# Gated delta rule as a scan of transition matrices, with the output projection's tiles in another order

## The chip, the cores and the metric

The kernel runs on one core of a Trainium2 chip. The metric is the device time of one execution in microseconds (us), lower is better. The core has a matrix engine (PE), a vector engine (DVE), a scalar engine (ACT), a GpSimd engine (POOL), and queues that start transfers (DMA), the main one on SP. Each engine runs its own list of instructions in order, and waits on semaphores for the others. Matrix products are written to PSUM banks; the kernel holds four banks with the tag `g` (psg) and four with the tag `m` (psm).

## What is computed

One layer of a hybrid decoder on 1024 tokens of width 1024, in float32: normalise, project, four mixers A to D of 256 channels each, an output projection added to x, then a SwiGLU block and a last normalisation. The change concerns mixer C, a gated delta rule in 16 chunks of 64 tokens and 4 heads, and what follows it.

```python
def chunk_gated_delta_rule(q, k, v, g, beta):
    ...
    kb = k * beta[..., None]
    low = jnp.where(strict, jnp.einsum('bhncd,bhnsd->bhncs', kb, k) * decay, 0.0)
    rhs = jnp.concatenate([v * beta[..., None], kb * jnp.exp(gc)[..., None]], axis=-1)
    sol = lax.linalg.triangular_solve(low, rhs, left_side=True, lower=True, unit_diagonal=True)
    u, w = sol[..., :dv], sol[..., dv:]
    ...
    def step(state, inp):
        qg_n, w_n, u_n, attn_n, kd_n, dec_n = inp
        v_new = u_n - jnp.einsum('bhcd,bhde->bhce', w_n, state)
        o = jnp.einsum('bhcd,bhde->bhce', qg_n, state) + jnp.einsum('bhcs,bhse->bhce', attn_n, v_new)
        state = state * dec_n[..., None, None] + jnp.einsum('bhcd,bhce->bhde', kd_n, v_new)
        return state, o
...
    mix = jnp.concatenate([y_a, y_b.astype(x.dtype), y_c, y_d], axis=-1)
    x = x + (mix @ w_out[l]).astype(x.dtype)
    x = x + swiglu(rmsnorm(x, norm2_w[l]), w_gate_up[l], w_down[l]).astype(x.dtype)
```

## The kernel before

Channels lie on the 128 partitions and tokens on the free axis, in two halves of 512 tokens. A large product is float32 made of three passes (`mm3`, L178 to L180): both operands are split into a rounded part and a rest (`wh` and `wl` for weights, made by ACT at L167 and DVE at L169; `mh` and `ml` for the mixers' outputs, L886 and L887). Such a pass is a matmul of 128x128 weights on 512 columns and is called a full matmul below. A column of weights is a generator in `queue`; `fill(us)` lets the queue put in some steps of three full matmuls, so that small work is interleaved with them. In which order the instructions then stand on each engine is decided when the program is built; the lists in the section on the change are from that order.

Mixer C needs small matmuls: 64x64, float32, on half of the partitions. Each is two records in the trace. Before the scan, a triangular inverse `Ti` is made per head and chunk: DVE solves blocks of 32 by substitution (L852, L853), transfers rearrange them (L868), and two sets of 32x32 matmuls (L932, L944) join them.

The scan (L1024 to L1078) goes through 16 chunks in turn. In each, PE multiplies the keys with the state (L1034), DVE adds the scaled result to the values (L1038), PE applies `Ti` (L1045), DVE copies the result (L1047), PE multiplies with the decayed keys (L1054) and makes two products per output (L1066, L1067), and DVE updates the state (L1060). That is up to 20 small matmuls in three places per chunk, 308 in all, with `fill(0.64)` after each place. The keys in channel order (`Kc`) come from a copy in DRAM (`dK`), which ACT's queue writes and POOL's queue reads.

The output projection is split: columns `o0` and `o1` (`col_out`, 8 per half, 18 full matmuls each, evacuated at L916) use the six blocks of mixers A, B and D and run beside the scan; columns `p0` and `p1` (`col_out2`, 4 per half, 2 x 6 full matmuls, evacuated at L983) add the two blocks of mixer C. After chunk 8 the first half's output is normalised (`onorm`, L591 to L613) and `p0` is put in the queue. Behind the scan come the statistics of the first half (`stats`, L152, with sums of squares in `acc2` that DVE adds at L989) and the split of the first half for the SwiGLU block (`split_h0`, L1017).

The SwiGLU block is done with Strassen-like products whose right sides are sums and differences of quarters of x. `sums_b(j)` (L1175 to L1184, lower parts at L1168) makes the sides T1, T2 and T4 from columns j and j+4 of both halves, and `sums_b2(j)` those of T3 and of the last quarter. The string `GQ` sets the order: n waits for a column, s and t are the sums, a and b are four products that need no sums. The first product that needs a sum is S2 of the first block. It reads T2, and weights that DVE makes (L1237) and ACT splits (L1120).

POOL multiplies `vtok` and `ktok` by per-token factors (L840), four instructions of 128x1024.

## Time and profile before

| | us |
|---|---|
| median of 3 runs | 1191.02 |
| lowest and highest run | 1187.15, 1191.15 |
| the profiled execution | 1191.06 |
| span of its trace | 1189.3 |
| PE busy | 1149.8 (97%) |
| DVE busy | 837.6 (70%) |
| ACT busy | 497.5 (42%) |
| POOL busy | 292.2 (25%) |

The span is from the first to the last instruction; 1.8 us of the profiled execution lie around it. Columns of the views: in a timeline, start, duration, engine, line, operation, output and input, count, and in brackets the idle time before it with what ended it. Matmuls overlap, so the distance of two starts, not the duration, is what one costs. [...]

### The profile page before, as it was taken

To read this page: it belongs to the slowest core of one execution; us is meant where nothing else is said; L and a number is where in the kernel's file an instruction comes from. 1 tells how busy PE (TensorE), PEld (TensorE's weight loads), DVE (VectorE), ACT (ScalarE), POOL (GpSimd) and SP (SyncE) were. 2 spreads that over 40 slices of the span, in tenths; PEclk is the share of its full clock that TensorE was granted. 3 is DMA by queue.
4 is the path that set the end of the run, shared out by engine and by line. 5 is a ranking of instruction groups with operands and counts; after the bars stand their busy time and mean duration, and the time that the engine had idled before them with its cause. 6 is when DMAs were issued, how large, how long until landed. Compare 5 with 4: busy or idle time off the path is not lost.

```text
span 1189.3 us, 17008 instructions
## 1 busy us (share of the span) xinstructions
PE 1149.8 (97%) x6426; PEld 931.0 (78%) x6426; DVE 837.6 (70%) x1419; ACT 497.5 (42%) x852; POOL 292.2 (25%) x232
## 2 busy tenths in 40 slices
PE   7999999989999899997999999999999999999996
PEld 6877777877787667775888888888888888888885
DVE  7656445377499346799866676576665679999876
ACT  7465335455322323457323233232323335436553
POOL 5200000011000200001275566465565510000004
PEclk9999999999999899998999999999999999999998
DMA  6121101211222712352132222131222299555103
GB/s 218 54 82 36 37 19 55 70 53 36 59 66 64 256 45 90 98 163 87 66 119 82 76 85 107 53 107 53 106 89 89 77 330 354 177 186 183 39 1 142
DMA packets 64115, 122.19 MB, mean 103 GB/s; under 512 B 16105, under 2 KB 22553, under 8 KB 64033
## 3 DMA queue, kind: packets, MB, share of 16 engines
q1 hardware_dynamic: 45488, 95.00, 24.4%
q10 hardware_dynamic: 16912, 20.34, 4.7%
q0 software_dynamic: 1632, 5.77, 1.3%
q8 instruction: 51, 0.84, 0.3%
q14 instruction: 32, 0.25, 0.1%
HBM read 98.48 MB, written 22.59 MB: 102 GB/s over the span
## 4 chain that ended last, share of the span: by engine, by line
PE 85%; DVE 8%; ACT 3%; DMA 2%; issue 1%; SPq 0%; DVEq 0%; ACTq 0%
PE psg L178 17%; PE psg L180 17%; PE psg L179 17%; PE psm L178 9%; PE psm L179 8%; PE psm L180 8%; ACT S L365 1%; DMA wr<-w_out 1%; DVE wl L169 1%; DMA t<-x 1%; DVE big L222 1%; PE psm L159 1%; PE psm L591 1%; DVE S L852 1%; PE psm L569 1%
## 5 line engine op out<-in xcount | busy, mean ns | idle before, releaser
L178 PE MATMUL psg<-big,wh 128*128 128x512 f32 x616 | 251.8, 409 | 1.0 <-ACT wh L167 1.0
L180 PE MATMUL psg<-big,wl 128*128 128x512 f32 x616 | 245.5, 399 | 4.9 <-DVE wl L169 4.9
L179 PE MATMUL psg<-big,wh 128*128 128x512 f32 x616 | 245.7, 399 | 0.3 <-DVE big L222 0.3
L180 PEld LDWEIGHTS psg<-big,wl 128*128 128x128 f32 x616 | 117.5, 191 | 32.1 <-DVE wl L169 6.4
L178 PEld LDWEIGHTS psg<-big,wh 128*128 128x128 f32 x616 | 117.5, 191 | 29.9 <-issue 4.1
L179 PEld LDWEIGHTS psg<-big,wh 128*128 128x128 f32 x616 | 117.8, 191 | 23.5 <-DVE big L222 0.8
L1121 DVE TENSOR_TENSOR wl<-S,wh 128x512 fp32r<-128x512 f32 x115 | 94.8, 834 | 28.2 <-ACT wh L1120 27.9
L167 ACT ACTIVATE wh<-wr 128x512 fp32r<-128x512 f32 (+2 forms) x104 | 58.3, 564 | 129.2 <-PE psg L179 98.5
L1120 ACT ACTIVATE wh<-S 128x512 fp32r<-128x512 f32 x115 | 70.7, 625 | 99.0 <-PE psm L179 36.3
L169 DVE TENSOR_TENSOR wl<-wr,wh 128x512 fp32r<-128x512 f32 (+2 forms) x104 | 64.3, 624 | 42.0 <-ACT wh L167 38.2
L1274 DVE TENSOR_TENSOR t<-t,t 128x512 f32<-128x512 f32 x44 | 41.9, 956 | 43.5 <-ACT t L1148 30.5
L1224 POOL TENSOR_TENSOR wr<-S 128x512 f32<-128x512 f32 x20 | 28.9, 1448 | 176.4 <-DVE r L146 158.3
L1298 POOL TENSOR_TENSOR t<-t,rstdb 128x512 f32<-128x512 f32 x40 | 55.4, 1407 | 37.1 <-DVE t L1294 37.1
L1495 POOL TENSOR_TENSOR big<-big,t 128x256 f32<-128x256 f32 (+1 forms) x9 | 8.0, 917 | 196.0 <-ACT t L1490 196.0
L1120 ACT ACTIVATE yB<-S 128x512 fp32r<-128x512 f32 x55 | 33.0, 623 | 48.0 <-PE psm L180 31.5
L1121 DVE TENSOR_TENSOR yA<-S,yA 128x512 fp32r<-128x512 f32 x51 | 40.0, 799 | 18.4 <-ACT yA L1120 17.8
L1121 DVE TENSOR_TENSOR yB<-S,yB 128x512 fp32r<-128x512 f32 x55 | 40.5, 758 | 14.7 <-ACT yB L1120 14.1
L1120 ACT ACTIVATE yA<-S 128x512 fp32r<-128x512 f32 x51 | 30.8, 623 | 48.0 <-PE psm L180 25.5
L1148 ACT ACTIVATE t<-t 128x512 f32<-128x512 f32 x22 | 13.9, 633 | 76.4 <-POOL t L1147 72.2
L1237 POOL TENSOR_TENSOR S<-S 128x512 f32<-128x512 f32 x20 | 26.8, 1341 | 74.6 <-DVE wl L1121 48.0
L1232 POOL TENSOR_TENSOR S<-wr,S 128x512 f32<-128x512 f32 x20 | 31.7, 1583 | 35.7 <-DVE wl L1121 26.3
L178 PE MATMUL psm<-big,wh 128*128 128x512 f32 x96 | 37.5, 391 | 0.0
(486 smaller groups left out, 2835.1 us busy)
## 6 DMA issues: line engine op xcount, KB each, us to landing
S<-w_gu SPq DMA_DIRECT2D x42, 512.0 KB, 3.7
wr<-w_in SPq DMA_DIRECT2D x48, 256.0 KB, 2.6
actd<-t ACTq DMA_DIRECT2D x22, 512.0 KB, 2.6
t<-w_down SPq DMA_DIRECT2D x22, 512.0 KB, 5.1
wr<-w_down SPq DMA_DIRECT2D x33, 256.0 KB, 3.9
wr<-w_out SPq DMA_DIRECT2D x24, 256.0 KB, 2.6
S<-actd SPq DMA_DIRECT2D x11, 512.0 KB, 6.1
big<-xd SPq DMA_DIRECT2D x4, 1024.0 KB, 8.7
```

Of the source, the lines that this page charges most:

```text
L167: act(hi, raw, AF.Copy)
L169: V.tensor_tensor(lo, raw, hi.bitcast(F32), SUB)
L178: mm(out, lhsT=w[0], rhs=hi, start=start, stop=False)
L179: mm(out, lhsT=w[0], rhs=lo, start=False, stop=False)
L180: mm(out, lhsT=w[1], rhs=hi, start=False, stop=stop)
L1120: act(hi, raw, AF.Copy)
L1121: V.tensor_tensor(lo, raw, hi.bitcast(F32), SUB)
L1224: early(f).tensor_tensor(r["S1"], r["A21"], r["A22"], ADD)
L1232: early(f).tensor_tensor(r["S2"], r["S1"], r["A11"], SUB)
L1237: early(f).tensor_tensor(r["S4"], r["A12"], r["S2"], SUB)
L1274: V.tensor_tensor(v[:, h, :], v[:, h, :], s[:, h, :], MUL)
L1298: early(f).tensor_tensor(v[:, h], v[:, h], rstdb[:, hs(h)], MUL)
```

## The change

The scan's state is made by one matrix per chunk: S(n+1) = M(n) S(n) + B(n), with M(n) = decay - W K and B(n) the offset. Five batches of 64 small matmuls each make these for all 32 pairs of heads and chunks at once: W (`Wc`), the solved values (in `vtok`), M (`Mt`), the offsets (in the states' tile `St`), and corrected queries (in `qg`). ACT evacuates three of them and DVE two, in groups of 128x512. The scan is then one product of 4 small matmuls and one DVE addition for each of 14 chunks, with one step of `fill`. The outputs of four chunks at a time are made by `outputs`, 28 or 32 small matmuls in one place. In all there are 500 small matmuls.

`dK` and its two transfers each way are gone. POOL multiplies `vtok` alone; DVE makes `K2`, `ktok` and `Mt`, two instructions of 128x1024 each, and a small identity (`id64`). The x tiles in the places S8 and S3 are loaded after the batches that use these places.

Of the output projection, `o0` runs beside the batches and the scan, then `p0`; the second half is done after that as eight columns `f1` (`col_all`, 24 full matmuls each, all eight blocks). `stats(0)` and `split_h0` stand under the first of them, and `sums_b` between them. The string `GQ` is changed for it.

```diff
-GM = (2.08, 2.64, 8.4, 3.56, 2.28)
-GS = (0.64, 0.64, 0.64)
+GM = (2.08, 2.64, 1.28, 2.56, 1.28)
+GS = (0.64,)
...
-GQ = 'n0 L0 s0 n1 n2 s2 q0 n3 a0 s1 L1 s3 t3 P0 a1 P1 t0 b0 t2 S0 b1 P2 t1'
+GQ = 'n0 s0 n1 s1 L0 n2 s2 q0 n3 a0 s3 L1 P0 a1 t0 P1 b0 t1 S0 b1 t2 P2 t3'
...
-    dK = dr.tile([2, P, T], F32, name="dK")
-    for hp in range(2):
-        nc.scalar.dma_start(out=dK[hp], in_=kq[hp][:, 0].rearrange("p n t -> p (n t)"))
...
-    for c in (slice(0, 16), slice(16, 32)):
-        for t, k in ((vtok, br), (ktok, kds)):
-            G.tensor_tensor(t[:, c, :], t[:, c, :], k[:, c].unsqueeze(2).broadcast_to([P, 16, 64]), MUL)
+    for c in groups:
+        G.tensor_tensor(vtok[:, c, :], vtok[:, c, :], by_tok(vtok, br, c), MUL)
...
+    def col_all(h, ct):
+
+        def steps(w):
+            p = psg()
+            for q, kt in enumerate(order + [4, 5]):
+                mm3(p, w(q), mh[h][:, kt, :], ml[h][:, kt, :], q == 0, q == 7)
+                if q == 5 and len(queue) > 1:
+                    queue[1].prep()
...
+            def evac():
+                add_x2(h, ct, p)
+                done_x2(h, ct)
...
     for ct in range(8):
         col_out(0, ct)
-    for ct in (0, 4, 1, 5, 2, 6, 3, 7):
-        col_out(1, ct)
+    K2 = S(8, [P, 32, 64])
+    for c in groups:
+        V.tensor_tensor(K2[:, c, :], ktok[:, c, :], by_tok(K2, nbeg, c), MUL)
+        V.tensor_tensor(ktok[:, c, :], ktok[:, c, :], by_tok(ktok, kds, c), MUL)
...
+    Mt = S(6, [P, 32, 64])
+    for c in groups:
+        V.tensor_tensor(Mt[:, c, :], bcu(id64, 16), by_tok(Mt, decC, c), MUL)
...
+    def batch(lhs, rhs, evac):
+        for g in range(4):
+            p = psm()
+            for q in range(8):
+                for r in half:
+                    mm(p[r, q * 64:(q + 1) * 64], lhsT=lhs[r, 8 * g + q, :], rhs=rhs[r, 8 * g + q, :],
+                       start=True, stop=True)
+            evac(g, p.rearrange("p (q c) -> p q c", c=64))
...
+    Wc = S(3, [P, 32, 64])
+    batch(Ti, K2, copy_to(Wc))
+    batch(Ti, vtok, copy_to(vtok))
     x_tile(S(8, [P, 2, T]))
+    fill(GM[3])
+    batch(Wc, ktok, add_to(Mt))
+    St = S(1, [P, 16, 2, 64])
...
+    batch(ktok, vtok, to_states)
+    batch(Wc, attnT, add_to(qg))
     x_tile(S(3, [P, 2, T]))
...
+    norm0 = onorm_steps(oC, 0, dnn, qs)
+    for n in range(1, 15):
+        p = psm()
+        for hp in range(2):
+            for r in half:
+                mm(p[r, hp * 64:(hp + 1) * 64], lhsT=Mt[r, hp * 16 + n, :], rhs=St[r, n, hp, :],
+                   start=True, stop=True)
+        V.tensor_tensor(St[:, n + 1], p[:, 0:P].rearrange("p (a c) -> p a c", a=2), St[:, n + 1], ADD)
+        if n in (3, 7, 11):
+            outputs(n // 4)
+        if n >= 8:
+            next(norm0, None)
+        fill(GS[0])
+    outputs(3)
...
+    split_c(0)
+    for j in range(4):
+        col_out2(0, j, len(queue))
+    onorm(oC, 1, dnn, qs, GO2)
+    split_c(1)
...
+    while queue:
+        step()
+    flush()
+    for ct in (0, 4, 1, 5, 2, 6, 3, 7):
+        col_all(1, ct)
+    queue[0].prep()
+    fill(2 * 0.64)
+    stats(0)()
+    for k in range(KT):
+        split_h0(k)
+        fill(0.64)
```

PE in the middle of the scan, before: the names are psg for a bank of the output projection, `big`, `wh`, `wl` for its operands, Sst for the state, t and vn for the values, S for the matrices.

```order
L1034 MATMUL psm_3744<-Sst_3721,S_538_3521 64x64 x4
L178 MATMUL psg_3717<-big_3297,wh_3686 128x512
L179 MATMUL psg_3717<-big_3298,wh_3686 128x512
L180 MATMUL psg_3717<-big_3297,wl_3688 128x512
L1045 MATMUL psm_3755<-t_586_3743,S_512_3287 64x64 x4
L178 MATMUL psg_3717<-big_3297,wh_3686 128x512
L179 MATMUL psg_3717<-big_3298,wh_3686 128x512
L180 MATMUL psg_3717<-big_3297,wl_3688 128x512
L1054 MATMUL psm_3777<-vn_3754,S_408_2385 64x64 x4
L1066 MATMUL psm_3742<-S_336_1961,Sst_3721 64x64
L1067 MATMUL psm_3742<-S_335_1960,vn_3754 64x64
```

The output products go on alternating behind these rows (L1066, L1067). The same place of the change (Mt and the states are both S tiles there):

```order
L176 MATMUL psg_3957<-big_3293,wh_3934 128x512
L177 MATMUL psg_3957<-big_3294,wh_3934 128x512
L178 MATMUL psg_3957<-big_3293,wl_3936 128x512
L1078 MATMUL psm_4010<-S_561_3781,S_530_3425 64x64 x4
L176 MATMUL psg_3957<-big_3293,wh_3934 128x512
L177 MATMUL psg_3957<-big_3294,wh_3934 128x512
L178 MATMUL psg_3957<-big_3293,wl_3936 128x512
L1078 MATMUL psm_4031<-S_561_3781,S_530_3425 64x64 x4
```

Three places of small matmuls per chunk, with outputs in the third, have become one, and the full matmuls between them are the same.

DVE ahead of product S2, before, from the evacuation of the last column of the projection (L983) on: wl and wr are weights, t and S the sums.

```order
L983 TENSOR_TENSOR S_540_3527<-psg_4878,S_540_3527 128x512
L989 TENSOR_TENSOR cB<-cB,t_840_4887 128x512
L1121 TENSOR_TENSOR wl_4925<-wr_4922,wh_4924 128x512
L1168 TENSOR_TENSOR S_815_4748<-t_827_4810,S_814_4747 128x512
L989 TENSOR_TENSOR cB<-cB,t_841_4892 128x512
L1121 TENSOR_TENSOR wl_4931<-wr_4928,wh_4930 128x512
L1224 TENSOR_TENSOR wr_4692<-praw_4689 128x512
L1175 SCALAR_TENSOR_TENSOR t_844_4911<-yA_3325,cA,t_844_4911 128x512
L1175 SCALAR_TENSOR_TENSOR t_851_4934<-yB_3328,cA,t_851_4934 128x512
L1176 SCALAR_TENSOR_TENSOR t_844_4911<-S_539_3524,cA,t_844_4911 128x512
L1183 SCALAR_TENSOR_TENSOR S_813_4746<-t_844_4911,S_812_4745 128x512
```

The sums for S2 go on behind these rows. DVE at the same place of the change, from the evacuation of the last f1 column (L921) on:

```order
L921 TENSOR_TENSOR S_570_3926<-psg_4927,S_570_3926 128x512
L1157 TENSOR_TENSOR wl_4997<-wr_4994,wh_4996 128x512
L1268 TENSOR_TENSOR praw_4634<-wr_4638,praw_4634 128x512
L916 TENSOR_TENSOR cB<-cB,t_767_4958 128x512
L1273 TENSOR_TENSOR praw_4634<-praw_4634 128x512
L1211 SCALAR_TENSOR_TENSOR t_770_4977<-yB_3324,cA,t_770_4977 128x512
L1157 TENSOR_TENSOR wl_5005<-praw_4634,wh_5004 128x512
L1212 SCALAR_TENSOR_TENSOR t_770_4977<-S_570_3926,cA,t_770_4977 128x512
L1219 SCALAR_TENSOR_TENSOR S_715_4678<-t_770_4977,S_714_4677 128x512
L1229 TENSOR_TENSOR t_783_5027<-t_783_5027 128x512
L1204 TENSOR_TENSOR S_713_4676<-t_770_4977,S_712_4675 128x512
```

In the first list 25 instructions stand from that L983 to the weights of S2 (L1237), in the second four from that L921 to them (L1273) and ten to the last lower part of T2 (the L1204 that writes S_713). On PE, 36 full matmuls stand between that column and S2 before, and 48 in the change.

DVE in the change where columns p0 end and the first f1 column begins (L921 evacuates, L916 adds squares, L167 makes the first weights of f1):

```order
L921 TENSOR_TENSOR yB_3324<-psg_4460,yB_3324 128x512
L916 TENSOR_TENSOR cB<-cB,t_663_4468 128x512
L921 TENSOR_TENSOR S_570_3926<-psg_4472,S_570_3926 128x512
L916 TENSOR_TENSOR cB<-cB,t_668_4486 128x512
L921 TENSOR_TENSOR yB_3324<-psg_4490,yB_3324 128x512
L916 TENSOR_TENSOR cB<-cB,t_670_4498 128x512
L921 TENSOR_TENSOR S_570_3926<-psg_4502,S_570_3926 128x512
L916 TENSOR_TENSOR cB<-cB,t_672_4510 128x512
L167 TENSOR_TENSOR wl_4528<-wr_4524,wh_4526 128x512
L916 TENSOR_TENSOR cB<-cB,t_673_4515 128x512
L916 TENSOR_TENSOR cB<-cB,t_674_4520 128x512
```

Before, the columns p0 stood among the scan's last chunks, and the weights that follow them were made beside it; now the weights of the first f1 column stand behind the last evacuation of p0.

## Rows read from the trace of the kernel before

**Rows 1.** The page: engines (busy, share, count); one group (busy, mean ns).

```profile
PE 1149.8 (97%) x6426; PEld 931.0 (78%) x6426; DVE 837.6 (70%) x1419; ACT 497.5 (42%) x852; POOL 292.2 (25%) x232
...
L1121 DVE TENSOR_TENSOR wl<-S,wh 128x512 fp32r<-128x512 f32 x115 | 94.8, 834 | 28.2 <-ACT wh L1120 27.9
```

**Rows 2.** Stretches: busy time and count of PE, PEld, DVE, ACT, POOL; PEclk; DMA.

```profile
375.00:400.00 25.00, 22.93 (x322) 18.47 (x321) 16.54 (x26) 13.73 (x26) 10.36 (x16) 0.86 0.66 221
...
525.00:550.00 25.00, 17.77 (x82) 14.19 (x80) 24.58 (x41) 18.21 (x32) 0.00 (x0) 0.93 0.19 63
550.00:575.00 25.00, 24.17 (x96) 19.19 (x97) 24.42 (x46) 12.67 (x23) 3.13 (x2) 0.87 0.28 90
```

**Rows 3.** Waits of PE, whole span: total, times, longest.

```profile
PE psg L178 <- ACT wh L1120: 7.3, 1, 7.3
...
PE psm L809 <- DVE S L815: 2.4, 1, 2.4
PE psm L1054 <- DVE vn L1047: 2.0, 1, 2.0
```

**Rows 4.** Timeline of PE in the scan.

```profile
423.61 0.45 PE L1034 MATMUL psm<-Sst,S 64*64 64x64 f32 x8
...
424.57 0.40 PE L180 MATMUL psg<-big,wl 128*128 128x512 f32 x1
...
425.61 0.39 PE L179 MATMUL psg<-big,wh 128*128 128x512 f32 x1
425.84 0.40 PE L180 MATMUL psg<-big,wl 128*128 128x512 f32 x1
...
427.39 0.39 PE L179 MATMUL psg<-big,wh 128*128 128x512 f32 x1
```

**Rows 5.** Timeline of PE in mixer D: full matmuls, then 32 small records.

```profile
139.83 0.39 PE L180 MATMUL psg<-big,wl 128*128 128x512 f32 x1
...
141.87 0.39 PE L180 MATMUL psg<-big,wl 128*128 128x512 f32 x1
142.19 1.15 PE L550 MATMUL psm<-t 64*64 64x64 f32 x32
```

**Rows 6.** Timeline of PE at L809, after its wait: two equal groups.

```profile
298.54 1.97 PE L809 MATMUL psm<-S 64*64 64x128 f32 x16
...
300.92 1.09 PE L809 MATMUL psm<-S 64*64 64x128 f32 x16
```

**Rows 7.** Three stretches, PE alone: length, busy time and count, PEclk, DMA.

```profile
389.40:395.90 6.50, 6.50 (x73) 0.50 0.85 292
406.40:409.80 3.40, 3.40 (x12) 0.50 0.43 163
550.60:556.60 6.00, 5.92 (x14) 0.50 0.81 286
```

**Rows 8.** Timeline of POOL and of DVE around 287 us.

```profile
284.99 3.77 POOL L840 TENSOR_TENSOR S<-S,tn 128x1024 f32<-128x1024 f32 x2 [13.17 <-ACT t L788]
...
287.20 2.10 DVE L169 TENSOR_TENSOR wl<-wr,wh 128x512 fp32r<-128x512 f32 x1
```

**Rows 9.** Timeline of DVE: a long multiply, the scan, the stretch before S2.

```profile
231.72 2.35 DVE L694 TENSOR_TENSOR S<-S,tn 128x1024 f32<-128x1024 f32 x2
...
396.42 0.69 DVE L169 TENSOR_TENSOR wl<-wr,wh 128x512 fp32r<-128x512 f32 x1 [5.38 <-ACT wh L167]
...
424.11 0.48 DVE L1038 SCALAR_TENSOR_TENSOR t<-psm,tn,S 128x64 f32<-128x64 f32 x2 [1.31 <-PE psm L1034]
...
425.39 0.29 DVE L1047 COPY vn<-psm 128x128 f32<-128x128 f32 x1 [0.81 <-PE psm L1045]
...
534.64 0.68 DVE L983 TENSOR_TENSOR S<-psg,S 128x512 f32<-128x512 f32 x1
...
550.05 0.68 DVE L1237 TENSOR_TENSOR praw<-praw 128x512 f32<-128x512 f32 x1
```

**Rows 10.** Timeline of ACT: the four evacuations of L944.

```profile
398.37 2.43 ACT L947 ACTIVATE S<-psm 32x512 f32<-32x512 f32 x4
```

More of the change, by code (lines that the diff above doesn't have):

```diff
@@ L582, in onorm, with onorm_steps @@
     def onorm(o, h, nw, qsum, gap):
+        for us, _ in zip(tuple(gap) + (0,), onorm_steps(o, h, nw, qsum)):
+            if us:
+                fill(us)
+    def onorm_steps(o, h, nw, qsum):
         sq = tl([P, 2, HT], "t4", 3)
         act(sq, o[:, :, hs(h)], AF.Square)
-        fill(gap[0])
+        yield
         p = psm()
@@ L602, in onorm @@
         V.tensor_tensor(r8[:, :, 1, :], rv, r8[:, :, 0, :], SUB)
-        fill(gap[1])
+        yield
         pT = psm()
@@ L608, in onorm @@
         act(row, pT[0:8, :], AF.Copy)
-        fill(gap[2])
+        yield
         for hp in range(2):
@@ L897, in trunk_kernel, with done_x2, add_x2 @@
     x_tile(tl([P, 2, T], "yB"))
+    acc2 = cB[:, 256:768]
+    xd = dr.tile([T, T], F32, name="xd")
+    def done_x2(h, ct):
+        xs = x2[ct][:, hs(h)]
+        if ct == 0:
+            act(acc2, xs, AF.Square)
+        else:
+            sq = tl([P, HT], "t4", 3)
+            act(sq, xs, AF.Square)
+            V.tensor_tensor(acc2, acc2, sq, ADD)
+        nc.scalar.dma_start(out=xd[ct * P:(ct + 1) * P, hs(h)], in_=xs)
+    def add_x2(h, ct, p):
+        xs = x2[ct][:, hs(h)]
+        V.tensor_tensor(xs, p, xs, ADD)
     def col_out(h, ct):
@@ L949, in trunk_kernel, with copy_to, add_to, to_states @@
     dmp("Ti", Ti)
-    Kc = S(6, [P, 2, 16, 64])
-    for hp in range(2):
-        G.dma_start(out=Kc[:, hp].rearrange("p n t -> p (n t)"), in_=dK[hp])
-    x_tile(S(8, [P, 2, T]))
+    fill(GM[2])
+    def batch(lhs, rhs, evac):
[6 more added lines that the diff above has]
+            evac(g, p.rearrange("p (q c) -> p q c", c=64))
+    def copy_to(t):
+        return lambda g, p: act(t[:, 8 * g:8 * g + 8, :], p, AF.Copy)
+    def add_to(t):
+        return lambda g, p: V.tensor_tensor(t[:, 8 * g:8 * g + 8, :], p, t[:, 8 * g:8 * g + 8, :], ADD)
+    Wc = S(3, [P, 32, 64])
+    batch(Ti, K2, copy_to(Wc))
+    batch(Ti, vtok, copy_to(vtok))
+    x_tile(S(8, [P, 2, T]))
+    fill(GM[3])
+    batch(Wc, ktok, add_to(Mt))
+    St = S(1, [P, 16, 2, 64])
+    def to_states(g, p):
+        hp, n = divmod(8 * g, 16)
+        k = min(8, 15 - n)
+        act(St[:, n + 1:n + 1 + k, hp, :], p[:, 0:k, :], AF.Copy)
+    batch(ktok, vtok, to_states)
+    batch(Wc, attnT, add_to(qg))
     x_tile(S(3, [P, 2, T]))
@@ new lines, in trunk_kernel, with outputs @@
+    oC = vtok.rearrange("p (a n) c -> p a (n c)", a=2)
+    def outputs(g):
+        p = psm()
+        pv = p.rearrange("p (a q c) -> p a q c", a=2, q=4)
+        for n in range(4 * g, 4 * g + 4):
+            for hp in range(2):
+                u = hp * 16 + n
+                for r in half:
+                    o = pv[r, hp, n % 4, :]
+                    mm(o, lhsT=vtok[r, u, :], rhs=attnT[r, u, :], start=True, stop=n == 0)
+                    if n > 0:
+                        mm(o, lhsT=St[r, n, hp, :], rhs=qg[r, u, :], start=False, stop=True)
+        act(oC[:, :, g * 256:(g + 1) * 256], p.rearrange("p (a t) -> p a t", a=2), AF.Copy)
@@ new lines, in trunk_kernel @@
+    norm0 = onorm_steps(oC, 0, dnn, qs)
+    for n in range(1, 15):
+        p = psm()
+        for hp in range(2):
+            for r in half:
+                mm(p[r, hp * 64:(hp + 1) * 64], lhsT=Mt[r, hp * 16 + n, :], rhs=St[r, n, hp, :],
[6 more added lines that the diff above has]
+        fill(GS[0])
@@ L996, in stats @@
+    outputs(3)
+    dmp("oC", oC)
+    for _ in norm0:
+        pass
+    split_c(0)
[3 more added lines that the diff above has]
+    split_c(1)
     def stats(h):
@@ L1081, in trunk_kernel @@
-    dmp("oC", oC)
-    need("p03")
-    onorm(oC, 1, dnn, qs, GO2)
-    split_c(1)
-    while trickle:
-        trickle.pop(0)()
-        fill(0.64)
-    stats(0)()
-    names = [c.name for c in queue]
-    for j in range(4):
-        at = [i + 1 for i, n in enumerate(names) if n in (f"o1{j}", f"o1{j + 4}", f"p1{j - 1}")]
-        at = at[-1] if at else 0
-        col_out2(1, j, at)
-        names.insert(at, f"p1{j}")
+    need("p03")
+    while queue:
[3 more added lines that the diff above has]
+        col_all(1, ct)
@@ L1313, in trunk_kernel @@
         if c == "n":
-            need(f"p1{j}")
+            need(f"f1{j + 4}")
         elif c == "q":
@@ L1641, in layout @@
     wo = wo.reshape(KT, P, KT, P)
-    d["w_out"] = np.stack([wo[[0, 1, 2, 3, 6, 7], :, j].transpose(1, 0, 2).reshape(P, -1) for j in range(8)])
+    d["w_out"] = np.stack([wo[[0, 1, 2, 3, 6, 7, 4, 5], :, j].transpose(1, 0, 2).reshape(P, -1) for j in range(8)])
     d["w_out2"] = np.stack([wo[4:6, :, j::4].transpose(1, 2, 0, 3).reshape(P, -1) for j in range(4)])
```

121 lines of the change are left out of this document (29 added, 92 removed).

## The prediction

> **What bounds the kernel now.** First the page: PE is busy for 97% of the span [rows 1], so time can come only from PE's own work, from its few waits, or from its clock. Then the stretches: the scan and what follows it hold most of what PE loses outside start and end. At 375 to 400 us it is idle for 2 us and its clock is granted at 0.86 on average; at 525 to 550 it is idle for 7 us while DVE is busy for 24.6 of 25 us; at 550 to 575 the clock is at 0.87 [rows 2]. The waits name the places [rows 3]: 7.3 us at product S2 for its weights, 2.4 us at L809, 2.0 us at the start of the scan. [...] So the change is worth what it does to PE's small matmuls, and to these waits with their tails. The sum is made against the profiled execution, 1191.06 us, which is the median of the runs to within 0.1 us.
>
> **Part 1, small matmuls on PE.** Nine full matmuls take 2.04 us, 0.227 each [rows 5]. Eight small records take 0.45 us [rows 4] and 32 take 1.15 [rows 5], so one more record costs 0.70 / 24 = 0.029 us, and a small matmul, two records, 0.058. In the scan, 424.57 to 425.61 holds two full matmuls and four small ones: 1.04 - 0.45 = 0.59 us for the four. 425.84 to 427.39 holds two full and twelve small: 1.55 - 0.45 = 1.10 [rows 4]. So one small matmul costs (1.10 - 0.59) / 8 = 0.064, and each place where full and small change over costs 0.59 - 4 x 0.064 = 0.33 on top. The order of before has the 308 small matmuls in 53 places, one of them beside other small work; the change has 500 in 16 places, four of them beside other small work. The change pays 192 x 0.061 = +11.7 us for matmuls and gets 40 x 0.33 = -13.2 for places. Sum **-1.5**, bounds -3 to +1: on PE alone the two forms are nearly equal. The 420 full matmuls from L932 to S2 are the same number in both.
>
> [...]
>
> **Part 2, the wait at S2.** Before, DVE is the late one. From the last evacuation of the projection (534.64) to the instruction that makes the weights of S2 (550.05) it runs 25 instructions without a gap in 15.4 us, 0.62 each [rows 9], and PE has only 36 full matmuls, 8.2 us, to run meanwhile. In the change PE has 48 full matmuls (10.9 us) between the last f1 column and S2, and DVE has four instructions ahead of the weights' sum and ten ahead of T2's last part, 6.8 us at that pace. Nor is DVE behind when it gets there: from the statistics of the first half to the last f1 column, 59 full and 9 short instructions (some 37 us) stand beside eight columns of 24 full matmuls (43.5 us). So the 7.3 us wait goes [rows 3], and with it the tail at the lower clock: 6.0 us at half speed [rows 7], of which up to 3.0 are lost; I take 2.7. If this cover failed, the 10.0 us would come back.
>
> **Part 3, the start of the scan.** The 2.0 us wait for L1047 [rows 3] and its tail of 3.4 us at 0.50 [rows 7], worth 1.4, have no successor: the chain from `Ti` through three small products and two DVE steps is replaced by batches, between which PE has full matmuls. Parts 2 and 3 together are 7.3 + 2.7 + 2.0 + 1.4 = **-13.4**. The low clock at 389.4 to 395.9 [rows 7] comes before the change's first instruction there and stays.
>
> **Part 4, POOL's two multiplies.** At 284.99 POOL multiplies `ktok` for 3.77 us, and the DVE instruction that starts at 287.20 takes 2.10 instead of 0.60 [rows 8]. DVE is then in one unbroken chain to the results that free the banks of L809, where PE waits 2.4 us [rows 3]. The change has no such POOL instruction there, so the chain ends 1.5 us earlier and the wait falls by as much. Behind that wait a group of L809 takes 1.97 us at the lower clock, and 1.09 at the higher [rows 6]; with the full matmuls among them the tail costs 1.5, and a wait of 0.9 may or may not still bring it. I take 1.4 + 0.8 = **-2.2**, bounds 0 to -2.9. DVE gets these multiplies back as `K2` and `ktok`, with `Mt` six of 1.18 us (2.35 for two [rows 9]), at 390 to 397 us, where before it idles for 5.4 us [rows 9]; the weights of the second column are pushed back by them, but PE has the two sets of 32x32 matmuls and the first batch to run meanwhile.
>
> **Part 5, new waits.** The first batch needs `Ti` from ACT, whose four evacuations take 2.43 us [rows 10] while PE runs on straight into the batch: 0.6 (0 to 1.5), and a clock that is still low there 0.5 (0 to 2). The batches give DVE and ACT one group of 16 matmuls (0.93 us) per evacuation of 0.6: nothing. In the scan a step costs PE 0.59 + 3 x 0.227 = 1.27 us; DVE starts 0.50 behind the start of PE's four (423.61 to 424.11 [rows 4, 9]) and needs some 0.3 for 128x128 (the copy of that size takes 0.29 [rows 9]), about 0.9 with its way back. It fits, except where a weight split or an evacuation (0.62) stands ahead: 0.5 in all (0 to 3). Where p0 ends, the first weights of f1 stand on DVE behind 21 instructions since the second half's normalisation, 22 x 0.62 = 13.6 us, against 53 full matmuls, 12.0: a wait of 1.5 (0 to 3.5) at the first f1 column. It also covers the sum of squares for `stats(0)`. The spread of those statistics needs seven short and five full DVE instructions, some 4.5 us, against 16 full matmuls, 3.6: 1.2 (0 to 2). Sum **+4.3**, bounds 0 to +12. The transfers of `dK` and the later x tiles cost nothing that PE sees: `dK` only filled queues, and the tiles are first read by evacuations some 20 us behind.
>
> **The sum.** -1.5 - 13.4 - 2.2 + 4.3 = -12.8, so 1191.1 - 12.8 = **1178.3 us**. All bounds at their best give about 1172, all at their worst 1191.
>
> **The rivals.**
>
> *The wait moves to p0.* DVE stays the bound, one stage earlier. For: p0 has an evacuation and an addition for every six full matmuls, 1.24 us of DVE against 1.36 of PE, and the normalisation comes on top. Where POOL works beside DVE, an instruction of this size takes 0.83 on average instead of 0.68 [rows 1]. Against: POOL has no work there in the order. At 0.77 per instruction the 22 take 16.9 us, a wait of 4.9, and with a tail at the lower clock of 2.7 the time is 1178.3 - 1.5 + 7.6 = 1184.4; with all 10.0 us of part 2 back it is 1186.8.
>
> *The scan's steps don't fit.* If every step had a 0.62 us instruction ahead of its addition, and this took 0.48 as the pair at L1038 does [rows 9], a step would need 1.7 instead of 1.27: 14 x 0.43 = 6 us, 1184. Against: in the order most steps have no such instruction ahead.
>
> *The clock falls in the batches: slower.* The batches are 29, 99 and 192 small matmuls with nothing between, up to 11 us without a full one. The one long run of small matmuls before, the 32x32 ones at 388 us, has the clock at 0.50 behind it [rows 7]. Were it so from the first batch to the scan, the small ones would take 1.97 / 1.09 = 1.81 times as long [rows 6], 320 x 0.058 x 0.81 = 15.0 us more, and the 31 full ones between them 7.0: 1178.3 + 22 = **1200**. It makes the kernel slower from some 13 us on, that is, if the low clock holds over more than half of it. Against: 64x64 matmuls stand among full ones over the whole scan, and one stretch at 298 us is half L809 at the low clock and comes out of it at full clock [rows 6]; and at 388 us PE had waited too. [...]
>
> [...]
>
> **How the numbers follow.** Forecast 0.76; the wait at p0 0.10; steps that don't fit 0.06; the low clock 0.06; matmuls that cost twice 0.02. A measurement of this kernel can tell about 0.5% from no change, so faster is below 1185.1, slower above 1197. Faster: 0.75 of the forecast, half of the wait at p0, and 0.04 of the steps, **0.84**. Same: what is left of these, and the doubled matmuls, **0.10**. Slower: **0.06**. The range is 1172 to 1186: all bounds at their best, and the two rivals that only give part of the gain back.
>
> **What would show it.** S2 without a wait, and no stretch at 0.50 behind it; no wait at the scan's start; L809's wait near 1 us. From the first 32x32 matmul to S2 it should be some 8 us shorter (parts 1, 2, 3 and 5 without the tail behind S2). Small matmuls 0.06 us apart in the batches and the clock at 1.00 there. One wait of 1 to 2 us for the first weights of f1. The prediction is wrong if PE waits at p0 or f1 for over 5 us, if the batches take over 25 us, or if L809 still waits 2.4.

## The result, and the profile after

The changed kernel took 1173.15 us (median of 4 runs, 1172.62 to 1175.18) where the kernel before took 1190.11 beside it: a ratio of 0.9865, 95% interval 0.9842 to 0.9887. Run again later beside other runs of before it gave 0.9873 (0.9849 to 0.9898). The forecast was 1178.3, a ratio of 0.9893. The direction and the range were right, and the gain was larger than forecast: 17.0 us between the medians and 18.4 between the two profiled executions (1191.06 and 1172.62) instead of 12.8.

First the page of the profile after, the first part, and then PE's longest waits over the whole span (line waited at, releaser: total, times, longest). The line numbers are those of the changed kernel: L176 to L178 were L178 to L180, L812 was L809, L993 was L932, and L1078 is the scan's step.

```profile
PE 1141.8 (98%) x6810; PEld 937.0 (80%) x6810; DVE 828.6 (71%) x1360; ACT 504.5 (43%) x860; POOL 287.8 (25%) x228
```

```profile
PE psg L178 <- DVE wl L167: 5.7, 3, 3.3
...
PE psm L993 <- DMA S<-dT: 1.2, 1, 1.2
PE psm L812 <- DVE S L818: 1.0, 1, 1.0
...
PE psm L1023 <- issue: 0.5, 2, 0.3
```

Against [rows 3]: the 7.3 us at S2 and the 2.0 at the scan's start are gone, and the 2.4 at L809 is 1.0. Of the three waits in the first row, the one of 3.3 and one of 0.9 were there before; the new one is this, at the first f1 column (timeline of PE: start, length of the record, the wait in brackets):

```profile
476.79 0.50 PE L178 MATMUL psg<-big,wl 128*128 128x512 f32 x1 [1.53 <-DVE wl L167]
```

The prediction had 1.5 there. Next the batches and three steps of the scan (timeline of PE), then the stretches (busy time and count of PE, PEld, DVE, ACT and POOL, the granted clock as a share of its higher level, DMA):

```profile
406.55 11.41 PE L1023 MATMUL psm<-S,S 64*64 64x64 f32 x384
...
425.68 0.45 PE L1078 MATMUL psm<-S,S 64*64 64x64 f32 x8
426.94 0.45 PE L1078 MATMUL psm<-S,S 64*64 64x64 f32 x8
428.21 0.45 PE L1078 MATMUL psm<-S,S 64*64 64x64 f32 x8
```

```profile
384.00:388.00 4.00, 4.00 (x128) 3.65 (x129) 4.00 (x7) 3.72 (x8) 3.50 (x6) 0.70 0.50 120
...
412.00:416.00 4.00, 4.00 (x146) 4.00 (x142) 0.69 (x1) 1.88 (x4) 0.00 (x0) 1.00 0.02 4
436.00:440.00 4.00, 4.00 (x22) 3.03 (x22) 1.17 (x4) 1.86 (x2) 0.00 (x0) 0.60 0.00 0
515.00:535.00 20.00, 20.00 (x94) 16.68 (x93) 19.05 (x33) 15.03 (x28) 0.00 (x0) 1.00 0.18 62
```

In the last batches 192 small matmuls are 384 records in 11.41 us, 0.0297 each, at full clock (1.00 from 412 to 416 us). A step of the scan takes 1.27 us, as forecast, and PE waits in none. Ahead of S2 (515 to 535) PE is never idle, where [rows 2] had 7 us. The one row that nobody forecast is 436 to 440: the clock is at 0.60, and PE had waited for nothing there (timeline of PE; L594 is the normalisation's 128x2 matmuls):

```profile
434.65 0.45 PE L1078 MATMUL psm<-S,S 64*64 64x64 f32 x8
435.03 1.99 PE L594 MATMUL psm<-hsel,t 128*128 128x2 f32 x16
436.88 0.77 PE L176 MATMUL psg<-big,wh 128*128 128x512 f32 x1
437.46 0.63 PE L177 MATMUL psg<-big,wh 128*128 128x512 f32 x1
```

The full matmuls behind L594 are 0.42 to 0.60 apart there, where 0.227 is their pace at full clock.

Where the 18.4 us went, by the starts of the same instructions in both traces:

| stretch | before | after | difference |
|---|---|---|---|
| start of the kernel to L809 / L812 | 284.76 | 283.31 | -1.4 |
| from there, with its wait and the tail behind it, to the first 32x32 matmul | 102.04 | 99.11 | -2.9 |
| first 32x32 matmul to S2's first product | 163.88 | 152.35 | -11.5 |
| from there to the end | 638.6 | 636.0 | -2.6 |

In the third stretch PE's idle time falls from 11.0 to 3.6 us. What PE loses to the lower clock (its busy time times one less the granted clock, summed over stretches of 2 us) falls from 5.1 to 3.4. The rest, PE's own work, is 2.4 us less.

### The profile page after: what moved, and what is told of

Same layout as the page of the kernel before. It is cut to its first block, busy times and chain, and to the rows that moved or that the text cites. A ratio compares the mean times of both kernels' runs of the same rounds, so it can differ in the third digit from the quotient of the medians.

```text
span 1170.8 us, 17683 instructions
## 1 busy us (share of the span) xinstructions
PE 1141.8 (98%) x6810; PEld 937.0 (80%) x6810; DVE 828.6 (71%) x1360; ACT 504.5 (43%) x860; POOL 287.8 (25%) x228
## 4 chain that ended last, share of the span: by engine, by line
PE 85%; DVE 8%; ACT 3%; DMA 1%; issue 1%; SPq 0%; DVEq 0%; ACTq 0%
PE psg L176 17%; PE psg L178 16%; PE psg L177 16%; PE psm L177 9%; PE psm L176 9%; PE psm L178 9%; PE psm L1023 2%; DVE S L859 1%; ACT S L363 1%; DVE S L860 1%; DMA t<-x 1%; PE psm L157 1%; DVE big L220 1%; PE psm L594 1%; DVE wl L167 1%
## 5 line engine op out<-in xcount | busy, mean ns | idle before, releaser
L178 PE MATMUL psg<-big,wl 128*128 128x512 f32 x616 | 244.0, 397 | 5.8 <-DVE wl L167 5.7
L176 PE MATMUL psg<-big,wh 128*128 128x512 f32 x616 | 248.7, 404 | 0.5 <-ACT wh L165 0.5
L177 PE MATMUL psg<-big,wh 128*128 128x512 f32 x616 | 243.8, 396 | 0.6 <-DVE big L220 0.6
L178 PEld LDWEIGHTS psg<-big,wl 128*128 128x128 f32 x616 | 117.1, 190 | 33.1 <-DVE wl L167 7.5
L176 PEld LDWEIGHTS psg<-big,wh 128*128 128x128 f32 x616 | 117.3, 190 | 29.7 <-issue 4.4
L165 ACT ACTIVATE wh<-wr 128x512 fp32r<-128x512 f32 (+1 forms) x100 | 57.3, 579 | 93.4 <-PE psg L177 61.9
L167 DVE TENSOR_TENSOR wl<-wr,wh 128x512 fp32r<-128x512 f32 (+1 forms) x100 | 63.6, 646 | 31.0 <-ACT wh L165 30.9
L1273 POOL TENSOR_TENSOR S<-S 128x512 f32<-128x512 f32 x20 | 27.4, 1372 | 72.9 <-DVE wl L1157 46.7
L176 PE MATMUL psm<-big,wh 128*128 128x512 f32 x96 | 37.5, 391 | 0.0
```

What stands on the lines that cost most here:

```text
L165: act(hi, raw, AF.Copy)
L167: V.tensor_tensor(lo, raw, hi.bitcast(F32), SUB)
L176: mm(out, lhsT=w[0], rhs=hi, start=start, stop=False)
L177: mm(out, lhsT=w[0], rhs=lo, start=False, stop=False)
L178: mm(out, lhsT=w[1], rhs=hi, start=False, stop=stop)
L1273: early(f).tensor_tensor(r["S4"], r["A12"], r["S2"], SUB)
```

## Experiments on the parts

**Part 4 alone, in the kernel before.** The multiply of `ktok` moves from POOL to DVE.

```diff
-        for t, k in ((vtok, br), (ktok, kds)):
-            G.tensor_tensor(t[:, c, :], t[:, c, :], k[:, c]..., MUL)
+        G.tensor_tensor(vtok[:, c, :], vtok[:, c, :], br[:, c]..., MUL)
...
+    for c in (slice(0, 16), slice(16, 32)):
+        V.tensor_tensor(ktok[:, c, :], ktok[:, c, :], kds[:, c]..., MUL)
```

> The kernel before, with part 4 of the change alone: the multiply of ktok by kds goes from POOL to DVE, where DVE idles behind the weights of the projection; the transfer of dK and everything else stay. Theory (POOL's multiply delays the DVE chain to the results that free the banks of L809): the DVE instruction that took 2.10 us beside it takes 0.60, PE's wait at L809 falls from 2.4 us to about 1.0, and with it the tail at the lower clock goes, so that between 1.4 and 2.9 us come off, 1190.1 - 2.9 = 1187.2 at best. Rival (the wait at L809 got shorter in the changed kernel through something else, the missing transfer of dK or an earlier start): the wait stays at 2.4 us and the time at 1190 within 0.5. Both: the two multiplies on DVE, 2.35 us, stand in its idle time and cost PE nothing.

Measured: 1181.75 us, ratio 0.9946 (0.9926 to 0.9966), so 4 to 9 us off and not 1.4 to 2.9. First DVE, then PE (timelines), where [rows 8] had 2.10 and [rows 6] a group of 1.97:

```profile
289.84 0.68 DVE L169 TENSOR_TENSOR wl<-wr,wh 128x512 fp32r<-128x512 f32 x1
...
291.72 1.22 DVE L924 TENSOR_TENSOR S<-S,tn 128x1024 f32<-128x1024 f32 x1
...
294.32 1.22 DVE L924 TENSOR_TENSOR S<-S,tn 128x1024 f32<-128x1024 f32 x1
```

```profile
299.86 1.09 PE L809 MATMUL psm<-S 64*64 64x128 f32 x16 [0.88 <-DVE S L815]
301.31 1.09 PE L809 MATMUL psm<-S 64*64 64x128 f32 x16
```

The instruction beside POOL is short again and the wait at L809 is down to 0.9 us, but not by the way that was expected. The two multiplies (L924) do not stand in idle time of DVE: the order of this build puts them into the very chain that PE waits for at L809. From the start of L169 to the first result (L815) it takes 9.46 us here and 8.53 in the kernel before. PE waits less because the build also gave it other work: 26 full matmuls stand ahead of the group that waits instead of 15, some 2.5 us more. So this run does not isolate what POOL's multiply costs.

Two other places changed as well. PE's waits from 375 to 560 us (the lines from here on are one higher than before: L1055 was L1054):

```profile
PE psg L178 <- ACT wh L1121: 7.2, 1, 7.2
PE psg L180 <- DVE wl L169: 2.4, 2, 1.8
PE psm L1055 <- DVE vn L1048: 0.7, 1, 0.7
```

At the 32x32 matmuls it is the order again. PE starts them at 388.52 us instead of 386.80: 0.4 us because the weights of the second column come later (the wait for them is 1.8 instead of 1.0), and 1.4 because 16 full matmuls stand behind that wait instead of 10. By then `dT` has landed, and the wait of 1.1 us for it is gone. At the scan's start 0.7 is left of 2.0. Was that chance? The same kernel and the kernel before were profiled once more.

> The kernel before with the multiply of ktok by kds on DVE, once more. Open from its first run: beside L809 it also lost the wait for dT at the first 32x32 matmuls with the 6.5 us at the lower clock behind it, and 1.3 us of the wait at the scan's start with its tail, some 6 us that the prediction did not give to this edit. Theory 1 (it is this edit's doing: the weights of the second column, pushed back on DVE, hold PE until dT has landed, and DVE is free sooner at the scan's start): both are missing again. Theory 2 (chance, as other stretches at the lower clock come and go in the same kernel): one of them is there again. Time: 1181 to 1184 by theory 1, 1184 to 1187 by theory 2.

> The kernel before, with nothing edited, profiled a second time, to see which of its stretches at the lower clock are there in every execution. Expected by both theories: the waits of 7.3 us at S2, 2.4 at L809 and 2.0 at the scan's start are there again within 0.3 us, since the program sets them. Theory 1 (each tail belongs to its wait): the clock is low behind all three again. Theory 2 (the tails come by chance): one is missing or at least 2 us shorter or longer, or the start of the kernel is without its stretch at 32 to 40 us.

Measured: 1185.43 us, ratio 0.9947 (0.9927 to 0.9967), and before 1190.57 in its one run. PE's waits from 375 to 560 us, first with part 4, then before:

```profile
...
PE psg L180 <- DVE wl L169: 2.4, 2, 1.8
PE psm L945 <- ACT S L936: 0.5, 2, 0.4
```

```profile
PE psg L178 <- ACT wh L1120: 7.3, 1, 7.3
PE psm L1054 <- DVE vn L1047: 2.8, 1, 2.8
PE psg L180 <- DVE wl L169: 1.7, 2, 1.0
PE psm L932 <- DMA S<-dT: 0.9, 1, 0.9
```

Both waits are missing a second time with part 4 and there a second time without it: they are the edit's doing, as theory 1 has it, though through the order that the build makes of it and only in small part through the weights. (The one at the scan's start came out at 2.8 instead of 2.0, outside the 0.3 that was expected.) Why DVE is in time at the scan's start was not taken apart. For the clock it is theory 2: behind the 32x32 matmuls, where [rows 7] has 0.50 for 6.5 us, the second execution of before has full clock, behind nearly the same wait:

```profile
388.00:392.00 4.00, 4.00 (x116) 3.58 (x109) 2.47 (x5) 3.55 (x8) 4.00 (x8) 1.00 0.60 174
```

**POOL's multiply put back in the changed kernel.**

```diff
         G.tensor_tensor(vtok[:, c, :], vtok[:, c, :], by_tok(vtok, br, c), MUL)
+        G.tensor_tensor(ktok[:, c, :], ktok[:, c, :], by_tok(ktok, kds, c), MUL)
```

> The changed kernel with POOL's multiply of ktok by kds put back at its old place, behind the vtok one; the two multiplies on DVE stay, so ktok is multiplied twice and the values of the states differ. Theory (POOL's multiply costs what the prediction's part 4 named, at L812 only): a DVE instruction of about 2.10 us beside it, the wait at L812 2.4 instead of 1.0 us and a tail at the lower clock behind it, together +2.9; 1174.5 (the mean of the changed kernel's two medians, 1173.2 and 1175.3) + 2.9 = 1177.4. Rival (part 4 is worth the 6 to 8 us by which it alone shortened the kernel before): 1180.5 to 1182.5, with a longer stretch at the lower clock around the 32x32 matmuls as well.

Measured: 1177.94 us, ratio 0.9888 (0.9871 to 0.9905). Against the changed kernel's 0.9865 and 0.9873 that is about 2 to 3 us, the theory's size and not the rival's, but the intervals overlap; the traces decide. DVE beside POOL's instruction, the same place in the changed kernel, then PE behind the wait (timelines):

```profile
290.24 2.10 DVE L167 TENSOR_TENSOR wl<-wr,wh 128x512 fp32r<-128x512 f32 x1
```

```profile
285.75 0.68 DVE L167 TENSOR_TENSOR wl<-wr,wh 128x512 fp32r<-128x512 f32 x1
```

```profile
299.33 1.09 PE L812 MATMUL psm<-S 64*64 64x128 f32 x16 [2.45 <-DVE S L818]
301.01 1.09 PE L812 MATMUL psm<-S 64*64 64x128 f32 x16
```

The 2.10 and the 2.45 us are back. Here the order is the same: 15 full matmuls stand ahead of the group in both kernels (and in the kernel before). From the start of L167 to the first result (L818) the chain takes 8.53 us instead of 7.12, and the wait is longer by the same 1.41. The tail is not back: both groups take 1.09 here. So the part is worth the wait at L812, and a tail that may or may not come; what else the kernel before gained from it came with the new order. The gains of the parts don't add up.

**The old projection order with the short scan.**

```diff
     for ct in range(8):
         col_out(0, ct)
+    for ct in (0, 4, 1, 5, 2, 6, 3, 7):
+        col_out(1, ct)
...
-        col_out2(0, j, len(queue))
+        col_out2(0, j, at + j)
...
-    for ct in (0, 4, 1, 5, 2, 6, 3, 7):
-        col_all(1, ct)
+        col_out2(1, j, at)
```

> The changed kernel with the batches and the short scan, but with the projection's tiles in the order of before: the columns o1 behind o0 in the queue, p0 ahead of the last eight of them, p1 put between the o1 columns. Theory 1 (the reordering is what covers DVE's work ahead of S2, as in part 2 of the prediction): the wait at S2 and its tail come back, 7.3 + 2.7 us, while the wait at f1 (1.5) goes: 1173.2 + 10.0 - 1.5 = 1181.7. Theory 2 (the short scan uses some 40 fewer fill steps, so these stand behind the scan and cover DVE in either order): from the spread of the statistics to S2 there are then 66 full matmuls, 15 us, against 21 DVE instructions, 13 us: a wait of 0 to 2 us at S2, and 1172 to 1176 in all.

Measured: 1178.6 us, ratio 0.9915 (0.9894 to 0.9937), between the two. PE's waits from 440 to 500 us, where p0 ends, and from 500 to 556, around S2:

```profile
PE psg L178 <- DVE wl L167: 2.1, 1, 2.1
PE psg L176 <- ACT wh L165: 0.7, 1, 0.7
```

```profile
PE psg L178 <- DVE wl L1159: 2.2, 2, 1.2
```

The 7.3 us do not come back: PE does not wait at S2, and two waits of 1.1 and 1.2 stand behind it, about what theory 2 counted. What theory 2 left out is the 2.8 us where p0 ends, with the clock at its lower level behind them for some 3 us (from 486.31 to 488.45 us the full matmuls start 0.42 to 0.43 apart instead of 0.227). The instructions counted in the traces say why. From the spread of the first half's statistics to S2, PE has 111 full matmuls in the kernel before, 192 here and 213 in the changed kernel; DVE has about the same work up to the weights of S2, 53, 57 and 56 instructions. Behind the last evacuation PE has 33 before and 36 here. So the wait at S2 falls mostly because the short scan leaves its full matmuls for behind it. This run keeps the new `GQ`; what the string does by itself was not tested. The reordering is worth the last 3 to 5 us (1178.6 against 1173.2 and 1175.3).

**The price of a small matmul, and the clock in a long run.**

```diff
-    batch(ktok, vtok, to_states)
+    for _ in range(4):
+        batch(ktok, vtok, to_states)
```

> The changed kernel with the fourth batch (ktok with vtok, to St) run four times instead of once, which writes the same values: 192 more 64x64 matmuls, and the run of small matmuls ahead of the scan is 384 instead of 192 long with no full matmul in it. Theory (a small matmul costs 0.059 us, and the clock stays up in a run of them): +192 x 0.059 = 11.3, so 1173.2 + 11.3 = 1184.5, and the clock granted at 1.00 through some 23 us. [...] Rival 2 (the clock falls where the run is long enough): the records from there on take 1.8 times as long, +11.3 to +20, and a stretch at about 0.50.

Measured: 1186.31 us (10 runs, ratio 0.9973). The run of small matmuls (timeline of PE) and a stretch of it:

```profile
410.99 22.61 PE L1023 MATMUL psm<-S,S 64*64 64x64 f32 x768
```

```profile
428.00:432.00 4.00, 4.00 (x145) 4.00 (x142) 0.91 (x2) 1.68 (x3) 0.00 (x0) 1.00 0.01 4
```

384 more records take 22.61 - 11.41 = 11.2 us, 0.029 each and 0.058 for a small matmul, as the theory has it. The clock is at 1.00 in this stretch, near the end of the run at 433.5 us, and the full matmuls behind the run start 0.23 apart. Rival 2 falls, for a run of 768 records. The whole is 13.2 us longer than the changed kernel's 1173.15 and 11.0 longer than its second median, 1175.27; the profiled execution also has 1.8 us more of waits for issue ahead of the batches.

**The price of a place where full and small matmuls change over.**

```diff
             evac(g, p.rearrange("p (q c) -> p q c", c=64))
+            if g < 3:
+                fill(0.64)
```

> The changed kernel with one fill step (three full matmuls) behind each of the first three groups of every batch, 15 steps, which are then missing later. Theory (each place where full and small matmuls change over costs 0.33 us, the term that pays for the 192 more small matmuls in part 1): the stretch from the batches' first matmul to the scan's first holds 45 more full matmuls, 45 x 0.227 = 10.2 us, and 15 more places, 5.0 us: 15.2 us longer. Rival (small matmuls cost the same wherever they stand, and the gain between L932 and S2 comes from the waits alone): 10.2 us longer. In the whole time the 10.2 us come back later except for what the missing cover costs at f1: DVE has 13.6 us of work there and PE then some 24 matmuls fewer, so a wait there of up to 7 us.

Measured: 1190.57 us in one run. In the batches (timeline of PE), each group of 32 records is now followed by three full matmuls:

```profile
408.58 1.15 PE L1023 MATMUL psm<-S,S 64*64 64x64 f32 x32
...
410.55 1.15 PE L1023 MATMUL psm<-S,S 64*64 64x64 f32 x32
```

One such round takes 1.97 us, of which 32 records are 0.94 and three full matmuls 0.68: a place costs 0.35, and [rows 4] had given 0.33. The stretch from the batches to the scan is 44.75 us instead of 27.42, 17.3 longer. In the order of this build it holds 54 more full matmuls, not 45, and 14 more places: by the rival 54 x 0.227 = 12.3 us, and the 5.0 that are left are 0.36 for each place. The theory has it. The loss in the whole time is as large, though 10.2 us were to come back later; that was in neither expectation. Stretches of 4 us, behind the 128x2 matmuls of L594:

```profile
456.00:460.00 4.00, 4.00 (x19) 2.84 (x19) 1.24 (x4) 2.13 (x3) 0.00 (x0) 0.53 0.00 0
460.00:464.00 4.00, 1.47 (x5) 0.68 (x4) 2.00 (x7) 0.84 (x2) 0.00 (x0) 0.50 0.24 72
...
472.00:476.00 4.00, 3.62 (x68) 3.43 (x66) 2.44 (x6) 1.26 (x2) 0.00 (x0) 0.50 0.02 4
```

The clock stays at 0.50 until 476 us, and PE lacks the fill steps with which it would have covered its waits there, the longest of 2.5 us. The full matmuls that were spent in the batches were the cover of the scan.

## Experiments on what is left

**The stretch at 436 us, and the changed kernel again.**

> The changed kernel once more, with nothing edited, as the measure for the three beside it and to see which of its stretches at the lower clock come back. Theory 1 (the clock falls behind the first 128x2 matmuls of the scan, L594, because of what PE runs there): the stretch at about 0.60 behind L594 is there again, and 1173 within 1. Theory 2 (it falls there by chance): it is missing, or of another length, and the profiled time differs by as much, up to 2 us. In both the start of the kernel may be some 2.4 us longer, as in three of the runs so far.

```diff
             next(norm0, None)
...
+            fill(GS[0])
+            next(norm0, None)
         fill(GS[0])
```

> The changed kernel with one more fill step (three full matmuls) in the scan's steps 8 to 14, between the step's four small matmuls and the piece of the normalisation, so that the 128x2 matmuls of L594 no longer follow other small ones. Theory (the clock falls because small and 128x2 matmuls stand together there): no stretch at the lower clock behind L594, 1.5 us less, and up to 0.33 for each of the few places where small work is now parted; 1172 to 1173. Rival (the 128x2 matmuls do it alone, or it is chance): the stretch stays and the time is 1173 to 1175. Seven fill steps, 4.8 us of full matmuls, are then missing behind the scan, where the wait at f1 could grow by as much if DVE is what it waits for.

Measured: the changed kernel again 1175.27 us (6 runs, 1170.62 to 1178.41), the edited one 1179.73 (ratio 0.9913, 0.9891 to 0.9934). First the changed kernel, then the edited one:

```profile
436.00:440.00 4.00, 4.00 (x26) 3.12 (x26) 1.94 (x6) 2.44 (x4) 0.00 (x0) 1.00 0.04 12
```

```profile
440.00:444.00 4.00, 4.00 (x24) 3.27 (x22) 1.64 (x5) 1.32 (x2) 0.00 (x0) 0.81 0.13 33
444.00:448.00 4.00, 4.00 (x22) 2.81 (x21) 1.26 (x7) 1.35 (x4) 0.00 (x0) 0.77 0.26 66
```

The same program has the stretch in one execution and not in the other, and with the matmuls parted it is still there. The theory that their standing together brings it has fallen; what decides it stays open. The edit itself costs 4 to 5 us, with intervals that just touch: there are more places, and PE's wait at the first f1 column grew from 1.5 to 2.6.

**The wait at f1, and all edits together.**

```diff
-    need("p03")
-    while queue:
-        step()
-    flush()
     for ct in (0, 4, 1, 5, 2, 6, 3, 7):
         col_all(1, ct)
-    queue[0].prep()
-    fill(2 * 0.64)
+    need("p03")
+    fill(4 * 0.64)
```

> The changed kernel with the f1 columns put into the queue before p0 has run out, so that the first f1 weights are split ahead of the last p0 evacuations on DVE, and with two more fill steps ahead of the statistics. Theory (PE's wait of 1.5 us at the first f1 column is DVE's queue ahead of that split): the wait falls to 0 to 0.5 us and nothing else grows, 1173.2 - 1.3 = 1171.9. Rival (DVE is behind there whatever its order, as the rival on p0 said): the wait moves to the statistics or to p0's own weights and the time stays at 1173 within 0.5.

> The changed kernel with the fill in front of the normalisation's pieces, the f1 weights early, and two more fill steps (six full matmuls, 1.4 us) ahead of the first 32x32 matmuls. Theory (the wait of 1.2 us for the transfer of dT there and the 2.5 us at the lower clock behind it go when PE comes 1.4 us later, and the three edits add up): -1.5 - 1.3 - 1.2 - 1.1 = -5.1, 1168.1. Rival (the fill steps are missed later, behind the scan, where nine fewer stand): waits at p0 or f1 give back up to 6 us, 1170 to 1174.

Measured: 1174.27 us (ratio 0.9867, 0.9844 to 0.9890) and 1176.18 (0.9875, 0.9854 to 0.9896), beside 1175.27 for the changed kernel. With the weights early PE waits from 470 to 490 us only for these:

```profile
PE psg L176 <- ACT wh L165: 0.8, 1, 0.8
PE psg L178 <- DVE wl L167: 0.2, 1, 0.2
```

The 1.5 us became 1.0, so half a microsecond and not 1.3; the time is the same within what can be told. All three together are no faster either: the wait for `dT` is still 1.2 us, because the added full matmuls came to stand between the 32x32 matmuls and not ahead of them, and the wait at f1 is 1.4. The gains do not add up, as the rival said, but the time is above the rival's 1170 to 1174 too; in the profiled execution the clock is at 0.50 from 388 to 400 us (its full matmuls start 0.42 to 0.59 apart).

**The scan without fill.**

```diff
         if n >= 8:
             next(norm0, None)
-        fill(GS[0])
+            fill(GS[0])
```

> The changed kernel without the fill step in the scan's steps 1 to 7, so that each of these is four small matmuls, DVE's addition and nothing else on PE; the seven fill steps run behind the scan instead. Theory (the prediction's estimate of the chain, 0.9 us from step to step): steps 1 to 7 start 0.9 us apart where nothing stands on PE between them, PE waits about 0.6 us in each for DVE's addition, some 4 us in all, and 7 places of 0.33 us are saved: +1.5 to +3, more where the clock falls. Rival (the chain is as long as the 1.27 us of a step with its fill, and only just fits): steps 1.2 us or more apart, waits of 0.9 each, +4 to +6.

Measured: 1172.39 us, ratio 0.9842 (0.9825 to 0.9858). The scan (timeline of PE):

```profile
420.29 0.45 PE L1078 MATMUL psm<-S,S 64*64 64x64 f32 x8
420.66 0.50 PE L176 MATMUL psg<-big,wh 128*128 128x512 f32 x1
...
421.56 0.45 PE L1078 MATMUL psm<-S,S 64*64 64x64 f32 x8
```

The edit did not make the steps bare: full matmuls of later fill steps moved up between them, and a step takes 1.27 us as before. It tells nothing on how long the bare chain is. The ratio is the best of all here, but its interval overlaps the changed kernel's. In the changed kernel DVE's addition (timeline of DVE) starts 0.49 us behind the step's first matmul at 425.68 and takes 0.29, which speaks for the estimate of 0.9 (first row below). Two bare steps do stand in the kernel with fill in its batches, at a clock of 0.50 (timeline of PE, second fence):

```profile
426.17 0.29 DVE L1080 TENSOR_TENSOR S<-psm,S 128x128 f32<-128x128 f32 x1 [2.67 <-PE psm L1078]
```

```profile
471.60 0.69 PE L1080 MATMUL psm<-S,S 64*64 64x64 f32 x8 [0.74 <-DVE S L1082]
472.67 0.69 PE L1080 MATMUL psm<-S,S 64*64 64x64 f32 x8 [0.38 <-DVE S L1082]
```

They start 1.07 us apart. DVE's addition starts 0.73 behind the first matmul there, 0.24 later than at full clock; less these 0.24 the bare step would take 0.83, an estimate.

## Why the prediction was right, and where it was not

**Part 1** (-1.5, bounds -3 to +1): right. PE's own work between the first 32x32 matmul and S2 is 2.4 us less in one profile of the changed kernel and 1.9 in the other. The record (0.029) and the place (0.33) measured 0.029 and 0.35 to 0.36 by themselves.

**Part 2** (-10.0): the size was right, 7.3 us at S2 and 2.6 behind it, the step that explained it only in part. It gave the wait to the order of the projection, 48 full matmuls instead of 36 ahead of S2. With the old order 36 stand there and the wait is gone all the same, so the step that failed is "the change has 48": what counted was the whole backlog of full matmuls that the short scan leaves behind it, 192 or 213 of them since the spread instead of 111. The order then saves the 2.8 us at p0's end and the 2.2 behind S2, for 1.5 at f1.

**Part 3** (-3.4): right for the changed kernel. With part 4 alone only 0.7 us of this wait or nothing was left, in another order of both engines.

**Part 4** (-2.2, bounds 0 to -2.9): the mechanism was right, and 2.9 came: 1.4 of wait and 1.5 of tail. The term that was mis-sized is the tail, 0.8 taken of 1.5; with the wait put back it did not return, so 0.8 for a tail that may not come was no bad price. The 0.60 us that the short instruction was given is the distance of two starts; its record is 0.68 long, and the chain became 1.41 shorter instead of 1.5. DVE gets its multiplies back where the prediction put them, from 385.6 to 392.5 us, and PE has no new wait there.

**Part 5** (+4.3): about right in sum, 3.7, and wrong in its pieces. The f1 weights cost 1.5, as worked out, the issue of the batches 0.5. The spread cost 0.2 at its largest wait there instead of 1.2 (its own terms, 4.5 against 3.6, give 0.9), and the scan nothing. In their place came 1.5 us of lower clock behind L594: from 436.88 to 440.38 PE ran six full and eight small records, which would take some 2.0 at full clock (0.59 + 6 x 0.227, an estimate). The second execution is without this lower clock and has 1.2 more of waits for issue: in these pieces the sum was luck.

**The rest of the difference.** The profiled execution of the changed kernel reached L812 1.4 us earlier, which it had gained in its first 46 us, ahead of anything that was changed; that was luck of the execution, since other runs of it have a longer start. From the first 32x32 matmul to S2 the prediction had some 8 us, and 11.5 came. And "the low clock at 389.4 to 395.9 stays" was a step that failed: it lasted about half as long, which is some 1.5 us of it, and it is no property of the program. It comes and goes, as the last section shows.

**The rivals.** The wait at p0: not in this kernel, but it is what the old order shows. The slower one, a clock that falls in the batches: no, in 11.4 and in 22.6 us of them (1.00 in the stretches of 4 us read in them). The scan's steps fit, at 1.27 us. The chance of 0.02 for matmuls that cost twice rests on a cost that no run shows; what the runs show is 0.0297 us for a record in 384 of them, and 0.029 for each of 384 more.

**The signs of being wrong.** The wait at f1 is 1.5 and the one at L812 1.0. By the letter the sign "the batches take over 25 us" came: from the first batch's first matmul to the end of the last it is 25.8 us, with 25 full matmuls between. The sign was set too low: 320 small matmuls at 0.058 and the 31 full ones of the prediction are 25.6 by its own prices, without a place.

## What to carry to other kernels

A wait goes when the engine that waits has more of its own work queued ahead of it: here the 7.3 us at S2 went when 192 or 213 full matmuls stood ahead of it since the spread instead of 111. Shortening a serial stage that had to be covered leaves the cover for the next stage, and that can be worth more than the stage itself, here 7.3 us against the 2.0 of the wait in the scan. Count the places where small and full matmuls change over as well as the matmuls: at 0.33 us each (0.35 to 0.36 when measured by itself), 40 places paid here for 192 more small matmuls at 0.058. An edit of one instruction can make the build order other work anew, as with the 26 full matmuls instead of 15 ahead of L809: before a difference is put down to the edit, count in both traces what stands ahead of each wait. And do not add up the gains of parts that end in the same wait.
